# A hybrid decoder layer: where the convolution and gate of an up feature tile's second half stand in the queues

## The chip, the cores and the metric

The kernel runs on one core of a Trainium2 chip. The metric is the device time of one execution in microseconds (us); lower is better. The kernel before was timed three times: 1341.37, 1335.03 and 1337.39 us, median 1337.39.

## What is computed

One decoder layer on 16 learned tokens and 1024 input tokens of width 1024: RMSNorm, an input projection, four heads of differential attention beside four HGRN2 heads, an output projection, a residual sum, and then a feed-forward block with a causal convolution of width 3 over the tokens. The change lies in that last block, whose reference is:

```python
def conv_ffn(a, w_up, conv_w, conv_b, w_down):
    u = a @ w_up                                   # (1040, 1024) @ (1024, 2 * 2816)
    u = lax.conv_general_dilated(
        u, conv_w[:, None, :].astype(u.dtype), window_strides=(1,),
        padding=[(CONV_WIDTH - 1, 0)], dimension_numbers=('NWC', 'WIO', 'NWC'),
        feature_group_count=C) + conv_b            # each feature by itself: 3 taps over the tokens
    gate, up = jnp.split(u, 2, axis=-1)
    return (jax.nn.gelu(gate, approximate=True) * up) @ w_down
```

All data are 32-bit floats. The kernel writes every matmul operand as a high part and a low part and sums three products (high by high, high by low, low by high).

## The kernel before

**Feature tiles.** The 2816 gate features and the 2816 up features are taken in 22 tiles (`ft`) of 128 gate features and the 128 up features that belong to them. The tokens are taken in two halves of 512 (`p` = 0 and 1; half 0 has two more columns, the edge that the convolution needs). Tiles 0 and 1 go through `plain_unit`, tiles 2 to 21 through `unit`, which saves an eighth of the matmuls: it splits features, tokens and the model width in two each and forms seven products of sums where the plain way has eight. One product of one half is 12 matmuls into a bank of PSUM, over a weight part `uh` or `ul` and a token part `t`.

**The steps of a unit.** `unit` is a generator with seven steps, and the main loop at the end of the quoted code runs step j for half 0, then for half 1, before it goes on to step j + 1. So TensorE's order is pa, pa, pb, pb, pc, pc, pb, pb, pa, pa, pb, pb, pc, pc: bank pb is added to three times (steps 1, 3 and 5), and between two visits lie two groups of 12. Between the visits VectorE reads the bank: after step 1 it makes `u2` from pb, after step 3 `u3` from pb; both are called u in the profile. TensorE may add to pb again only when VectorE has read it. Step 3 of half 0 thus waits for the first `u2`, step 5 of half 0 for the first `u3`. `ug` (gate) and `uu` (up), 514 columns of one half, are filled in steps 3 to 6.

**Convolution and gate.** At the end of step 6 `gated` runs for that half. For the gate side and for the up side `conv` copies two columns from the half before (ScalarE), makes `c` with the third tap and the bias (ScalarE, ACTIVATE) and adds the other two taps (VectorE, two SCALAR_TENSOR_TENSOR). Then come the gelu of the gate side (ScalarE, ACTIVATE c<-c), the product of both sides (POOL, line 1280), and the store to `gsc` in DRAM (SP's queue, line 1281). The down projection later reads `gsc`.

**Weights.** In step j of tile ft, `prep` makes the parts of product j of tile ft + 1: loads into `ra` (line 1159), sums of weight blocks `ws` on POOL (line 1163), a cast to `uh` on ScalarE, and `ul` on VectorE or, for steps 2, 4 and 6, on POOL (line 155). A part is needed one tile after it is made, and its buffer is free when step j - 1 of the current tile is through.

**What sets the order.** TensorE's order is the program's. On the other engines a scheduler puts the instructions in order by priority when the kernel is built, and each engine runs its queue strictly in that order. `behind(name)` lets the instructions in its block be placed only behind a marked instruction of the same engine. Instructions of VectorE and ScalarE are recorded by a helper and have line 53 in the profile, so they are told apart by their tiles. Early in the up phase the first operands `gh` and `gl` of the down projection are made from `gi`, a load of `gsc`: two in the queues of tile 2 and one each in those of tiles 3 and 4.

Of the kernel before, what the change touches and what calls it, by code (L numbers as in the profile page):

```python
# [13 lines left out]
ALU = mybir.AluOpType  # L14
# [71 lines left out]
def layer_kernel(ctx: ExitStack, tc: tile.TileContext, x, meta, table, lbl, gpre, gpost, win,  # L86
# [17 lines left out]
    def close(*cms):  # L104
        for cm in cms:
            cm.__exit__(None, None, None)
# [957 lines left out]
    @contextmanager  # L1064
    def behind(*names):
        with ExitStack() as st:
            for nm in names:
                st.enter_context(tc.issue_after(marks[nm].ins))
            yield
# [191 lines left out]

    last = {}

    def conv(ft, p, side, u):
        m = ft + NF * side
        w = 2 * HALF
        if p:
            A.copy(u[:, :2], last[side][:, w:])
        last[side] = u
        c = cv.tile([P, w], F32, tag=f"c{side}", name=f"c{side}_{ft}_{p}", bufs=2 if side else 3)  # L1270
        A.activation(c, u[:, 2:2 + w], AF.Identity, bias=cbt[:, m:m + 1], scale=cwt[:, m, 2:3])
        V.scalar_tensor_tensor(c, u[:, 1:1 + w], cwt[:, m, 1:2], c, ALU.mult, ALU.add)
        V.scalar_tensor_tensor(c, u[:, 0:w], cwt[:, m, 0:1], c, ALU.mult, ALU.add)
        return c

    def gated(ft, p, ug, uu):
        cg = conv(ft, p, 0, ug)
        A.activation(cg, cg, AF.Gelu_apprx_tanh)
        cu = conv(ft, p, 1, uu)
        G.tensor_tensor(cg, cg, cu, op=ALU.mult)  # L1280
        st = SY.dma_start(gsc[P * ft: P * (ft + 1), 2 * HALF * p:2 * HALF * (p + 1)], cg)
        if ft == p == 0:
            marks["store"] = st

    def plain_unit(ft, p, bank):
        us = outputs(ft, p)
        e = EDGE[p]
        for col in range(2):
            a, n = ((2 - e, HALF + e), (2 + HALF, HALF))[col]
            for side in range(2):  # L1290
                pt = bank(f"pq{ft}_{p}_{col}{side}")[:, :n]
                for kh in range(2):
                    hi, lo = plain[ft, f"{side + 1}{kh + 1}"]
                    th, tl = tt[p][(0, 4, 7, 6)[2 * col + kh]]
                    for k in range(4):
                        s = slice(P * k, P * (k + 1))
                        T.matmul(pt, hi[:, s], th[:, k], start=(kh + k == 0), stop=False)
                        T.matmul(pt, hi[:, s], tl[:, k], start=False, stop=False)
                        T.matmul(pt, lo[:, s], th[:, k], start=False, stop=(kh == 1 and k == 3))
                A.copy(us[side][:, a:a + n], pt)  # L1300
                yield
        with behind("turned"):
            gated(ft, p, *us)
        yield

    def unit(ft, p, bank):
        nm = f"{ft}_{p}"
        ug, uu = outputs(ft, p)
        e = EDGE[p]
        x1 = xup.tile([P, HALF + 2], F32, tag="x1", name=f"x1_{nm}")[:, 2 - e:]  # L1310
        u2, u3 = (xup.tile([P, HALF], F32, tag=t, name=f"{t}_{nm}") for t in ("u2", "u3"))

        def mm(j, pt, first):
            hi, lo = made[7 * ft + j]
            th, tl = tt[p][j]
            pt = pt[:, HALF + e - width(p, j):]
            for k in range(4):
                s = slice(P * k, P * (k + 1))
                T.matmul(pt, hi[:, s], th[:, k], start=(first and k == 0), stop=False, skip_group_check=True)  # L1319
                T.matmul(pt, hi[:, s], tl[:, k], start=False, stop=False, skip_group_check=True)  # L1320
                T.matmul(pt, lo[:, s], th[:, k], start=False, stop=(k == 3), skip_group_check=True)  # L1321

        pa = bank(f"pa{nm}")[:, :HALF + e]
        mm(0, pa, True)
        A.copy(x1, pa)
        yield
        pb = bank(f"pb{nm}")[:, :HALF + e]
        mm(1, pb, True)
        V.tensor_tensor(u2, pb[:, e:], x1[:, e:], op=ALU.add)
        yield  # L1330
        pc = bank(f"pc{nm}")[:, :HALF + e]
        mm(2, pc, True)
        yield
        mm(3, pb, False)
        V.tensor_tensor(u3, pb[:, e:], x1[:, e:], op=ALU.add)
        V.tensor_tensor(uu[:, 2 + HALF:], pc[:, e:], u3, op=ALU.add)
        yield
        mm(4, pa, False)
        A.copy(ug[:, 2 - e:2 + HALF], pa)
        yield  # L1340
        mm(5, pb, False)
        V.tensor_tensor(uu[:, 2 - e:2 + HALF], pb, x1, op=ALU.add)
        yield
        mm(6, pc, False)
        V.tensor_tensor(ug[:, 2 + HALF:], pc[:, e:], u2, op=ALU.add)
        gated(ft, p, ug, uu)
        yield

    free = [ps_in("pq0"), ps_in("pq1")]
# [52 lines left out]
    for ft in range(2, NF):  # L1402
        units = [unit(ft, p, ps_b) for p in range(2)]
        for j in range(7):
            prep(7 * (ft + 1) + j)
            for u in units:
                next(u)
    close(t2_cm, t_cm, v_cm, xu_cm, mx_cm)

    f_cm, fp = pool("fin", 1)  # L1410
# [279 lines left out]
```

## Time and profile before

| | us |
|---|---|
| median of three runs | 1337.39 |
| the profiled execution | 1337.54 |
| its span in the trace | 1335.8 |
| TensorE busy | 1288.8 |
| VectorE busy | 914.6 |
| ScalarE busy | 690.3 |
| POOL busy | 414.1 |

The span runs from the first to the last instruction; 1.74 us of the profiled execution lie outside it. Times in the rows are us from the start of the span. A timeline row gives start, duration, engine, line, operation and tiles, with x and a count where rows in a row are merged; what stands in square brackets is the idle time of the engine ahead of it and what ended that. The names L1319, L1320 and L1321 are the three matmuls of a product in `unit`. The feature loop of `unit` runs from about 705 to 1113 us; 840 us is in tile 7, and a tile is about 19.9 us long.

### The profile page before, as it was taken

How to read it: one execution, taken by the hardware profiler on the slowest of the kernel's cores; microseconds unless marked ns; L12 is line 12 of the kernel's file. 1: busy time of each engine (PE TensorE's matmuls, PEld its weight loads, DVE VectorE, ACT ScalarE, POOL GpSimd, SP SyncE). 2: the span in 40 equal slices, each digit the busy share in tenths (PEclk: the TensorE clock that was granted, in tenths of full speed). 3: DMA queues.
4: the chain of work that ended last, by engine and by line, in shares of the span. 5: the costliest groups of instructions: out<-in, count | busy, mean ns of one | idle time of the engine just before them, and what ended most of it. 6: DMA issues, size and time to landing. Idle time of an engine off the chain costs nothing. (4 is left out here: it accounts for less than half of the span.)

```text
span 1335.8 us, 26319 instructions
## 1 busy us (share of the span) xinstructions
PE 1288.8 (96%) x10227; PEld 1191.1 (89%) x10227; DVE 914.6 (68%) x1589; ACT 690.3 (52%) x1670; POOL 414.1 (31%) x324
## 2 busy tenths in 40 slices
PE   6999999999999999999898999999999999999997
PEld 5898899989999999777798999999999998888886
DVE  7666657564756465836788787877777776697587
ACT  7365356534654565446655454454454454454454
POOL 3211211121202110122157566666657641010021
PEclk9999999999999999999998999999999999999999
DMA  6331333132311112826512222223222225964363
GB/s 215 108 125 60 104 101 122 52 128 92 115 36 34 32 33 66 259 96 231 187 64 88 95 73 82 84 76 115 80 82 78 80 80 177 330 218 154 107 205 119
DMA packets 84371, 153.07 MB, mean 115 GB/s; under 512 B 9571, under 2 KB 19843, under 8 KB 84246
## 3 DMA queue, kind: packets, MB, share of 16 engines
q1 hardware_dynamic: 84246, 151.39, 34.1%
q8 instruction: 80, 1.31, 0.4%
q14 instruction: 45, 0.37, 0.1%
HBM read 112.69 MB, written 38.67 MB: 113 GB/s over the span
## 5 line engine op out<-in xcount | busy, mean ns | idle before, releaser
L1319 PE MATMUL pb<-t,uh 128*128 128x258 f32 (+1 forms) x480 | 136.9, 285 | 8.1 <-DVE u L53 8.1
L1320 PE MATMUL pb<-t,uh 128*128 128x258 f32 (+1 forms) x480 | 135.6, 283 | 0.0
L1321 PE MATMUL pb<-t,ul 128*128 128x258 f32 (+1 forms) x480 | 135.6, 283 | 0.0
L1503 PE MATMUL pd<-wl,gh 128*128 128x512 f32 (+1 forms) x314 | 122.2, 389 | 0.3 <-DVE wl L53 0.2
L1504 PE MATMUL pd<-wh,gl 128*128 128x512 f32 (+1 forms) x314 | 122.1, 389 | 0.0
L1502 PE MATMUL pd<-wh,gh 128*128 128x512 f32 (+1 forms) x314 | 122.0, 388 | 0.0
L53 DVE SCALAR_TENSOR_TENSOR c<-uu,cwt,c 128x512 f32<-128x512 f32 x88 | 94.9, 1079 | 20.2 <-ACT c L53 19.5
L1280 POOL TENSOR_TENSOR c<-c,c 128x512 f32<-128x512 f32 x44 | 66.9, 1520 | 132.0 <-ACT c L53 123.6
L1319 PEld LDWEIGHTS pb<-t,uh 128*128 128x128 f32 x480 | 91.6, 191 | 9.2 <-DVE u L53 8.9
L1321 PEld LDWEIGHTS pb<-t,ul 128*128 128x128 f32 x480 | 92.0, 192 | 0.0
L1320 PEld LDWEIGHTS pb<-t,uh 128*128 128x128 f32 x480 | 91.4, 190 | 0.0
L1319 PE MATMUL pa<-t,uh 128*128 128x258 f32 (+1 forms) x320 | 90.2, 282 | 0.0
L1320 PE MATMUL pa<-t,uh 128*128 128x258 f32 (+1 forms) x320 | 89.9, 281 | 0.0
L1321 PE MATMUL pc<-t,ul 128*128 128x256 f32 x320 | 89.9, 281 | 0.0
L1319 PE MATMUL pc<-t,uh 128*128 128x256 f32 x320 | 89.9, 281 | 0.0
L1320 PE MATMUL pc<-t,uh 128*128 128x256 f32 x320 | 89.9, 281 | 0.0
L1321 PE MATMUL pa<-t,ul 128*128 128x258 f32 (+1 forms) x320 | 89.7, 280 | 0.0
L53 DVE SCALAR_TENSOR_TENSOR c<-ug,cwt,c 128x512 f32<-128x512 f32 x88 | 86.4, 982 | 1.8 <-ACT c L53 1.1
L1503 PEld LDWEIGHTS pd<-wl,gh 128*128 128x128 f32 x314 | 59.2, 189 | 13.9 <-DVE wl L53 1.0
L1504 PEld LDWEIGHTS pd<-wh,gl 128*128 128x128 f32 x314 | 59.3, 189 | 12.8
L1502 PEld LDWEIGHTS pd<-wh,gh 128*128 128x128 f32 x314 | 59.3, 189 | 12.8
L155 POOL TENSOR_TENSOR ul<-ws,uh 128x512 fp32r<-128x512 f32 x40 | 58.2, 1454 | 35.4 <-ACT uh L53 31.6
(411 smaller groups left out, 4205.2 us busy)
## 6 DMA issues: line engine op xcount, KB each, us to landing
ra<-in_wup_dram SPq DMA_DIRECT2D x80, 256.0 KB, 2.7
wd<-in_wdown_dram SPq DMA_DIRECT2D x44, 256.0 KB, 4.6
tsc<-wd SPq DMA_DIRECT2D x44, 256.0 KB, 2.9
gsc<-c SPq DMA_DIRECT2D x44, 256.0 KB, 2.0
wi<-tsc SPq DMA_DIRECT2D x44, 256.0 KB, 2.8
gi<-gsc SPq DMA_DIRECT2D x33, 256.0 KB, 3.6
wi<-in_wdown_dram SPq DMA_DIRECT2D x33, 256.0 KB, 3.4
msc<-mm SPq DMA_DIRECT2D x21, 256.0 KB, 3.5
```

The source lines that it names most:

```text
L53: ins = call(*args, **kw)
L155: (eng or G).tensor_tensor(lo, raw, hi.bitcast(F32), op=ALU.subtract)
L1280: G.tensor_tensor(cg, cg, cu, op=ALU.mult)
L1319: T.matmul(pt, hi[:, s], th[:, k], start=(first and k == 0), stop=False, skip_group_check=True)
L1320: T.matmul(pt, hi[:, s], tl[:, k], start=False, stop=False, skip_group_check=True)
L1321: T.matmul(pt, lo[:, s], th[:, k], start=False, stop=(k == 3), skip_group_check=True)
L1502: T.matmul(py, gh[:, s], wh, start=(k == 0 and pr not in (3, 7)), stop=False, skip_group_check=True)
L1503: T.matmul(py, gh[:, s], wl, start=False, stop=False, skip_group_check=True)
L1504: T.matmul(py, gl[:, s], wh, start=False, stop=(k == NH - 1), skip_group_check=True)
```

## The change

`seam` takes the copies of the two columns out of `conv`, so that they stay at the end of the half. The rest of `gated` for half 1 of tiles 2 to 21 goes on a list. `gate_waiting` runs what is on the list: after step 1 of the next tile has been issued, and placed behind that tile's last `u2` on VectorE; for the last tile, after the loop. Half 0 and the tiles of `plain_unit` keep their place.

```diff
+    def seam(p, us):
+        for side in range(2):
+            if p:
+                A.copy(us[side][:, :2], last[side][:, 2 * HALF:])
+            last[side] = us[side]
+
     def conv(ft, p, side, u):
         m = ft + NF * side
         w = 2 * HALF
-        if p:
-            A.copy(u[:, :2], last[side][:, w:])
-        last[side] = u
...
+    waiting = []
+
+    def gate_waiting():
+        with behind("u2"):
+            while waiting:
+                gated(*waiting.pop(0))
...
+        seam(p, us)
         with behind("turned"):
             gated(ft, p, *us)
...
-        V.tensor_tensor(u2, pb[:, e:], x1[:, e:], op=ALU.add)
+        marks["u2"] = V.tensor_tensor(u2, pb[:, e:], x1[:, e:], op=ALU.add)
...
-        gated(ft, p, ug, uu)
+        seam(p, (ug, uu))
+        if p:
+            waiting.append((ft, p, ug, uu))
+        else:
+            gated(ft, p, ug, uu)
         yield
...
             for u in units:
                 next(u)
+            if j == 1:
+                gate_waiting()
+    gate_waiting()
```

TensorE's instructions stand in the same order in both kernels. The order of the others is shown at the change from tile 5 to tile 6, which every later tile repeats. In the names c_5_1 is c of tile 5, half 1; the first u_6_0 and u_6_1 are `u2` of the halves of tile 6, the second u_6_0 is `u3` of half 0.

VectorE before, from the convolution of half 1 to the first `u3`:

```order
L53 SCALAR_TENSOR_TENSOR c_5_1_9446<-uu_1_9220,cwt,c_5_1_9446 128x512 x2
L53 SCALAR_TENSOR_TENSOR c_5_0_9415<-ug_0_9200,cwt,c_5_0_9415 128x512
L53 TENSOR_TENSOR ug_1_9219<-pc_1_9289,u_5_1_9222 128x256
L53 SCALAR_TENSOR_TENSOR c_5_0_9415<-ug_0_9200,cwt,c_5_0_9415 128x512
L53 TENSOR_TENSOR ul_9453<-ra_11_9454,uh_9452 128x512
L53 SCALAR_TENSOR_TENSOR c_5_1_9440<-ug_1_9219,cwt,c_5_1_9440 128x512 x2
L53 TENSOR_TENSOR ul_9505<-ws_9506,uh_9504 128x512
L53 TENSOR_TENSOR u_6_0_9469<-pb_0_9510,x_6_0_9468 128x256
L53 TENSOR_TENSOR u_6_1_9488<-pb_1_9524,x_6_1_9487 128x256
L53 TENSOR_TENSOR ul_9569<-ws_9570,uh_9568 128x512
L53 TENSOR_TENSOR u_6_0_9470<-pb_0_9510,x_6_0_9468 128x256
```

VectorE in the changed kernel, the same stretch (c_5_1_9527 is the gate side of half 1, c_5_1_9532 its up side):

```order
L53 SCALAR_TENSOR_TENSOR c_5_0_9415<-ug_0_9189,cwt,c_5_0_9415 128x512
L53 TENSOR_TENSOR ul_9442<-ra_11_9443,uh_9441 128x512
L53 SCALAR_TENSOR_TENSOR c_5_0_9415<-ug_0_9189,cwt,c_5_0_9415 128x512
L53 TENSOR_TENSOR ul_9494<-ws_9495,uh_9493 128x512
L53 TENSOR_TENSOR u_6_0_9458<-pb_0_9499,x_6_0_9457 128x256
L53 TENSOR_TENSOR u_6_1_9477<-pb_1_9513,x_6_1_9476 128x256
L53 SCALAR_TENSOR_TENSOR c_5_1_9527<-ug_1_9208,cwt,c_5_1_9527 128x512
L53 SCALAR_TENSOR_TENSOR c_5_1_9532<-uu_1_9209,cwt,c_5_1_9532 128x512
L53 SCALAR_TENSOR_TENSOR c_5_1_9527<-ug_1_9208,cwt,c_5_1_9527 128x512
L53 SCALAR_TENSOR_TENSOR c_5_1_9532<-uu_1_9209,cwt,c_5_1_9532 128x512
L53 TENSOR_TENSOR ul_9569<-ws_9570,uh_9568 128x512
L53 TENSOR_TENSOR u_6_0_9459<-pb_0_9499,x_6_0_9457 128x256
```

The four steps of half 1 have moved from ahead of the two `u2` to between them and the `ul` of step 3, which stands ahead of `u3`.

POOL before, around the two gate products:

```order
L1163 TENSOR_TENSOR ws_9570<-ra_11_9454,ra_21_9458 128x512
L1280 TENSOR_TENSOR c_5_0_9415<-c_5_0_9415,c_5_0_9420 128x512
L1280 TENSOR_TENSOR c_5_1_9440<-c_5_1_9440,c_5_1_9446 128x512
L155 TENSOR_TENSOR ul_9539<-ws_9462,uh_9538 128x512
L1163 TENSOR_TENSOR ws_9664<-ra_12_9460,ws_9506 128x512
L1163 TENSOR_TENSOR ws_9728<-ra_21_9724,ra_22_9722 128x512
L1163 TENSOR_TENSOR ws_9772<-ws_9728,ra_11_9720 128x512
```

POOL in the changed kernel, where the gate product is line 1283:

```order
L1163 TENSOR_TENSOR ws_9570<-ra_11_9443,ra_21_9447 128x512
L1283 TENSOR_TENSOR c_5_0_9415<-c_5_0_9415,c_5_0_9420 128x512
L155 TENSOR_TENSOR ul_9539<-ws_9451,uh_9538 128x512
L1163 TENSOR_TENSOR ws_9664<-ra_12_9449,ws_9495 128x512
L1163 TENSOR_TENSOR ws_9717<-ra_21_9713,ra_22_9711 128x512
L1283 TENSOR_TENSOR c_5_1_9527<-c_5_1_9527,c_5_1_9532 128x512
L1163 TENSOR_TENSOR ws_9761<-ws_9717,ra_11_9709 128x512
```

One `ul` and two `ws` have moved ahead of the product of half 1.

ScalarE before, from the cast of the first weights on:

```order
L53 CAST uh_9452<-ra_11_9454 128x512
L53 COPY x_6_0_9468<-pa_0_9471 128x258
L53 ACTIVATE c_5_1_9440<-ug_1_9219,cbt,cwt 128x512
L53 ACTIVATE c_5_0_9415<-c_5_0_9415 128x512
L53 COPY x_6_1_9487<-pa_1_9490 128x256
L53 CAST uh_9504<-ws_9506 128x512
L53 ACTIVATE c_5_1_9440<-c_5_1_9440 128x512
L53 CAST uh_9538<-ws_9462 128x512
L53 CAST uh_9568<-ws_9570 128x512
```

ScalarE in the changed kernel:

```order
L53 CAST uh_9441<-ra_11_9443 128x512
L53 ACTIVATE c_5_1_9527<-ug_1_9208,cbt,cwt 128x512
L53 COPY x_6_0_9457<-pa_0_9460 128x258
L53 ACTIVATE c_5_0_9415<-c_5_0_9415 128x512
L53 COPY x_6_1_9476<-pa_1_9479 128x256
L53 CAST uh_9493<-ws_9495 128x512
L53 CAST uh_9538<-ws_9451 128x512
L53 ACTIVATE c_5_1_9527<-c_5_1_9527 128x512
L53 CAST uh_9568<-ws_9570 128x512
```

The gelu of half 1 has gone behind one cast (step 2's weights) and still stands ahead of the cast of step 3's. On SP's queue the order is the same at this place; in tiles 3 and 4 the load `gi` has gone ahead of the store of half 1.

## The prediction

> **What bounds the kernel now.** I read the page first, then TensorE's waits by stage, then the timelines of all engines over one feature tile. The page gives TensorE nearly the whole span:
>
> ```profile
> PE 1288.8 (96%) x10227; PEld 1191.1 (89%) x10227; DVE 914.6 (68%) x1589; ACT 690.3 (52%) x1670; POOL 414.1 (31%) x324
> ```
>
> The change acts from tile 3 on, which begins after 724 us. What TensorE waits for is listed for the up phase from 640 us, and then again from 724 us alone:
>
> ```profile
> PE pb L1319 <- DVE u L53: 8.1, 4, 6.3
> ...
> PE pb L1319 <- DVE u L53: 1.8, 3, 0.7
> ```
>
> Of the 8.1 us, 6.3 are one wait in tile 2, before any gate of `unit` has been moved. What the change can still reach is three waits of 1.8 us. In the stage's steady part TensorE is never idle (columns: window, length, then busy time of PE, PEld, DVE, ACT and POOL):
>
> ```profile
> 800.00:1080.00 280.00, 280.00 (x2371) 279.81 (x2370) 214.40 (x311) 138.44 (x269) 180.41 (x127) 1.00 0.25 84
> ```
>
> The clock is granted in full there (1.00), and VectorE is busy for 214 of 280 us. So this stage is bound by TensorE's own rate, with a few nicks, all at the start of a pb group:
>
> ```profile
> 761.89 0.28 PE L1321 MATMUL pc<-t,ul 128*128 128x256 f32 x1
> 762.84 0.39 PE L1319 MATMUL pb<-t,uh 128*128 128x256 f32 x1 [0.66 <-DVE u L53]
> 763.06 0.28 PE L1320 MATMUL pb<-t,uh 128*128 128x256 f32 x1
> ...
> 769.25 0.40 PE L1319 MATMUL pb<-t,uh 128*128 128x258 f32 x1 [0.56 <-DVE u L53]
> ...
> 784.22 0.39 PE L1319 MATMUL pb<-t,uh 128*128 128x256 f32 x1 [0.54 <-DVE u L53]
> ...
> 823.93 0.37 PE L1319 MATMUL pb<-t,uh 128*128 128x256 f32 x1
> 824.13 0.28 PE L1320 MATMUL pb<-t,uh 128*128 128x256 f32 x1
> ...
> 1062.38 0.37 PE L1319 MATMUL pb<-t,uh 128*128 128x256 f32 x1
> ```
>
> Those at 762.84 and 784.22 follow a pc group: step 3 waits for `u2`. The one at 769.25 follows pa (its group has 258 columns): step 5 waits for `u3`, behind the down projection's `gl`. From 823.93 to 1062.38 every second tile, seven in all and 39.7 us apart (so a tile is 19.9 us long), shows a small catch at `u2`: no idle time, but a first matmul of 0.37 instead of 0.28.
>
> **What the change removes.** At a free start matmuls follow each other by 0.12 us (763.06 is 0.22 after 762.84, the catch; the rest by 0.12). At 762.84 the step is 0.95 instead of 0.12, so 0.83 are lost, 0.17 more than the idle time printed, and 0.10 with the next one: 0.93. At 784.22 by the same rule 0.54 + 0.17 + 0.10 = 0.81. The seven catches cost 0.20 - 0.12 = 0.08 each, 0.6 together. All of it hangs on `u2`: 0.93 + 0.81 + 0.6 = 2.3 us. It goes if `u2` comes earlier by 0.8 us or more.
>
> VectorE over one such tile shows what `u2` stands behind:
>
> ```profile
> 835.49 2.23 DVE L53 SCALAR_TENSOR_TENSOR c<-uu,cwt,c 128x512 f32<-128x512 f32 x2
> 837.64 0.74 DVE L53 SCALAR_TENSOR_TENSOR c<-ug,cwt,c 128x512 f32<-128x512 f32 x1
> 838.30 0.41 DVE L53 TENSOR_TENSOR ug<-pc,u 128x256 f32<-128x256 f32 x1
> ...
> 839.29 0.68 DVE L53 TENSOR_TENSOR ul<-ra,uh 128x512 fp32r<-128x512 f32 x1
> 839.89 2.44 DVE L53 SCALAR_TENSOR_TENSOR c<-ug,cwt,c 128x512 f32<-128x512 f32 x2
> 842.26 0.68 DVE L53 TENSOR_TENSOR ul<-ws,uh 128x512 fp32r<-128x512 f32 x1
> 842.86 0.74 DVE L53 TENSOR_TENSOR u<-pb,x 128x256 f32<-128x256 f32 x2
> 844.65 1.52 DVE L53 TENSOR_TENSOR ul<-ws,uh 128x512 fp32r<-128x512 f32 x1 [1.05 <-ACT uh L53]
> 846.10 0.41 DVE L53 TENSOR_TENSOR u<-pb,x 128x256 f32<-128x256 f32 x1
> ...
> 838.20 0.28 PE L1319 MATMUL pb<-t,uh 128*128 128x258 f32 x1
> ...
> 841.04 0.28 PE L1319 MATMUL pc<-t,uh 128*128 128x256 f32 x1
> ...
> 843.87 0.28 PE L1319 MATMUL pb<-t,uh 128*128 128x256 f32 x1
> ...
> 849.54 0.28 PE L1319 MATMUL pb<-t,uh 128*128 128x258 f32 x1
> ```
>
> The last four rows are TensorE's dates: pb of step 1 from 838.20 to 841.04 for both halves, step 3 from 843.87, step 5 from 849.54. The first `u2` ends at 842.86 + 0.41 = 843.27, 0.6 ahead of its date. By the order before, the pairs at 835.49 and 839.89 are the four convolution steps of half 1; the change takes them from in front of it.
>
> **What it adds: the same four between `u2` and `u3`.** Here POOL decides. POOL's and ScalarE's rows of the same stretch:
>
> ```profile
> 834.77 1.62 POOL L1163 TENSOR_TENSOR ws<-ra,ra 128x512 f32<-128x512 f32 x1
> 840.22 1.57 POOL L1280 TENSOR_TENSOR c<-c,c 128x512 f32<-128x512 f32 x1 [3.83 <-ACT c L53]
> 843.08 1.30 POOL L1280 TENSOR_TENSOR c<-c,c 128x512 f32<-128x512 f32 x1 [1.29 <-ACT c L53]
> 844.33 1.30 POOL L155 TENSOR_TENSOR ul<-ws,uh 128x512 fp32r<-128x512 f32 x1
> 845.71 1.62 POOL L1163 TENSOR_TENSOR ws<-ra,ws 128x512 f32<-128x512 f32 x1
> ...
> 835.66 0.82 ACT L53 ACTIVATE c<-ug,cbt,cwt 128x512 f32<-128x512 f32 x1 [1.01 <-DMA ra<-in_wup_dram]
> 836.46 0.62 ACT L53 CAST uh<-ra 128x512 fp32r<-128x512 f32 x1
> 837.04 0.38 ACT L53 COPY x<-pa 128x258 f32<-128x258 f32 x1
> 842.37 0.63 ACT L53 ACTIVATE c<-c 128x512 f32<-128x512 f32 x1 [1.46 <-DVE c L53]
> 844.00 0.62 ACT L53 CAST uh<-ws 128x512 fp32r<-128x512 f32 x1 [0.49 <-PE pc L1320]
> ```
>
> VectorE's `ul` takes 0.68 alone (839.29), but 1.52 at 844.65, where POOL runs from 844.33 to 845.63: it ends at 846.17, 0.54 after POOL. POOL's next, begun at 845.71, takes 1.62 instead of 1.30. The `u` at 846.10, which reads PSUM, keeps its 0.41 beside it. So a VectorE instruction with both operands in SBUF and a POOL instruction go one after the other, and the one held ends about 0.54 after POOL. The Trainium skill says the same in "SBUF — State Buffer", section "SBUF: two separate sides": the two share a port pair under an exclusive lock, and whoever starts first has it for the whole instruction. The rows agree. By that rule the moved steps lose the shelter that they have now: ahead of the gate product POOL sits idle for 3.83 us, in which they run; behind `u2` its queue is full.
>
> I lay the tile out again by these durations, in the new order. The gate sum of half 1 (`ug`, now at 838.30) no longer stands behind the convolution and is free at 835.6, when its bank is complete: two groups of 1.42 ahead of 838.20, and 0.2 to 0.3 more, since the last matmul is 0.28 long and begins 0.12 before the next group. ScalarE makes c of half 0 by 836.48, then a cast, then c of half 1 by 837.8. VectorE's two steps of half 0 run from 836.5 and 837.8, alone, since POOL's `ws` is over at 836.39. The gelu follows at 838.5, POOL's product from 839.2 to 840.5. The `ul` of step 1's weights (cast over by about 840.0) is held behind it to 841.05. The first `u2` runs from 841.0 to 841.4, 1.9 earlier than now; the second, free when its group is over (841.04 and 0.3 by the same count), to 841.7. The 2.3 us go.
>
> Now the four. The first runs from 841.7 to 842.4, alone. POOL's `ul`, whose cast must wait for step 1's last matmul (841.04) and is over by 841.8, comes in behind it; the second is held to 843.95, the third behind `ws` to 845.6, the fourth behind the other `ws` to 847.25. The gelu of half 1 goes after the third, to 846.3; the cast of step 3's weights stands behind it, to 846.9; their `ul` on VectorE runs 847.2 to 847.9, since POOL has just taken up the product. The first `u3` ends at 848.2. TensorE wants it at 849.5: 1.3 us to spare, in this parity of tiles. In the other `u2` is now 0.5 later against TensorE (its catches), so about 0.8 to spare. I therefore put the cost at nothing: 19 tiles (3 to 21) hide it behind the matmuls of steps 3 and 4. If the cover goes, each loses what `u3` is late.
>
> **The two tiles with `gl`.** Its rows:
>
> ```profile
> 767.58 1.28 DVE L53 TENSOR_TENSOR gl<-gi,gh 128x512 fp32r<-128x512 f32 x1 [3.16 <-ACT gh L53]
> 768.78 0.41 DVE L53 TENSOR_TENSOR u<-pb,x 128x256 f32<-128x256 f32 x1
> ```
>
> Here VectorE waited 3.16 us for a load that SP had queued behind the store of half 1. In the new order it stands ahead of that store, and the product of half 0 is 1 us earlier, so the wait shrinks; in its place `gl` comes after the four. It adds 0.7 to 1.6 ahead of `u3`, whose spare time is 0.8 to 1.3: between nothing and 0.8 lost, against 0.56 + 0.17 + 0.10 = 0.83 now in tile 4. I take the middle, about 0.4 in each of the two tiles, which equals the 0.83: no change, with 0.8 either way.
>
> **The other queues moved past.** POOL makes the product of half 1 at about 847.3 instead of 843.08, and one `ws` sum and what follows move back by up to a product's 1.30; they make weights for the next tile, 19.9 us on. SP stores half 1 some 4 us later, at 848.7:
>
> ```profile
> 841.82 2.91 SPq L1281 DMA_DIRECT2D gsc<-c  x2
> 851.34 0.88 SPq L1159 DMA_DIRECT2D ra<-in_wup_dram  x2
> ```
>
> The next load in that queue goes out at 851.34 and isn't held up. `ug` and `uu` of half 1 are read until 847.25; ScalarE overwrites that buffer after step 4 of half 1, behind 849.5. The copies of two columns only leave `conv`. The last tile's gate, after the loop, stands in the order where it stood, so the start of the down projection is unchanged.
>
> **Sum.** 1337.5 (the profiled execution) - 2.3 + 0 = 1335.2 us. The median, 1337.4, lies 0.15 below that execution, which changes nothing. This is 0.2% faster; about 0.5%, 6.7 us here, is what a measurement can tell from no change, so I forecast "the same".
>
> **The rivals.**
> *No gain.* The waits of 2.3 us come back at `u3`, for instance 0.1 us in each of 19 tiles and 0.4 more in the two with `gl`: 2.7 us. For it speaks that spare time of 0.8 is less than one more hold (about 0.9); against it that 0.8 is still spare. About 1337.9.
> *Slower: POOL holds all five.* In my layout POOL holds three of the five SBUF instructions (the four and the `ul`) between `u2` and `u3`. If it holds all five, each takes about 1.6 (the second of the pair at 839.89 took 2.44 - 0.74 = 1.7, the `ul` 1.52): 841.7 + 8.0 + 0.4 = 850.1, 0.6 after 849.5. Nineteen tiles lose 11 us: 1337.5 - 2.3 + 11 = 1346. It decides from two more holds in a tile. For it speaks the exclusive order in the rows; against it that POOL's next instruction after the two `ws` is the product, which must wait for the fourth step itself, so that POOL pauses just there.
> *More gain.* The 6.3 us in tile 2 go as well. The rows of the queues up to that place are the same in both kernels, so nothing shortens the wait. 1335.2 - 6.3 = 1329.
>
> **Chances.** Forecast 0.73, no gain 0.14, slower 0.10, more gain 0.03. Range: the runs before reached 2.4 below and 4.0 above their median; from 1335.2 that and the 0.8 of `gl` give 1332.0 to 1340.0, and for a part of the holds (0.1 to 0.2 a tile) I go on to 1341.0; the slower case lies outside. Faster by over 0.5% holds the last rival and a little of the scatter, 0.04; slower 0.10; the same 0.86.
>
> **What would show it.** Right: TensorE's waits from 724 us fall from 1.8 to under 1 us, none of them after a pc group; POOL's idle time ahead of its gate products falls, its product of half 1 comes about 4 us later in the tile; `u2` ends some 2 us ahead of step 3; the wait of 6.3 us stays. Wrong: a wait of TensorE at pb after a pa group in every tile, behind VectorE steps of 1.5 us and more; or TensorE waiting for `uh` or `ul`; or a feature tile whose length isn't 19.8 to 19.9 us.

## The result, and the profile after

Four runs of the changed kernel gave 1347.55 to 1357.81 us, median 1352.61; four of the kernel before 1335.03 to 1341.50, median 1339.38. The ratio is 1.0106 (95% interval 1.0067 to 1.0144): slower by about 1.1%, where the forecast was 0.2% faster. The profiled execution took 1347.55 us, with a span of 1345.7.

The feature loop alone shows more than the span. Its first matmul and the first of the down projection, in the trace of before:

```profile
705.22 0.29 PE L1319 MATMUL pa<-t,uh 128*128 128x258 f32 x1
...
1113.44 0.40 PE L1502 MATMUL pd<-wh,gh 128*128 128x512 f32 x1
```

The same two in the trace of after:

```profile
700.50 0.29 PE L1330 MATMUL pa<-t,uh 128*128 128x258 f32 x1
...
1123.42 0.40 PE L1520 MATMUL pd<-wh,gh 128*128 128x512 f32 x1
```

That is 408.2 us before and 422.9 after: 14.7 more. The span grew by 9.9 only, because this execution reached the loop 4.7 us earlier. That start lies between 700 and 710 us in the traces of this study, whatever is done inside the loop, so the loop's length is used below beside the ratios. (Counted from these starts, the tile shown at 840 us is tile 8 in both kernels, not tile 7.)

TensorE's waits from 724 us in the changed kernel (us in all, times, longest):

```profile
PE pb L1330 <- DVE u L53: 13.4, 17, 1.0
```

and its steady window (columns as in the prediction):

```profile
800.00:1080.00 280.00, 268.50 (x2252) 265.67 (x2251) 220.30 (x296) 124.96 (x254) 176.44 (x122) 1.00 0.24 79
```

TensorE, idle for nothing in this window before, is idle for 11.5 of 280 us at the same clock of 1.00. From 724 us on, all these waits lie at one place of the tile, between steps 4 and 5:

```profile
838.87 0.28 PE L1330 MATMUL pc<-t,uh 128*128 128x256 f32 x1
...
847.25 0.28 PE L1332 MATMUL pa<-t,ul 128*128 128x256 f32 x1
848.42 0.40 PE L1330 MATMUL pb<-t,uh 128*128 128x258 f32 x1 [0.88 <-DVE u L53]
```

The pa group ends at 847.25, and the pb group (258 columns: step 5) starts 1.17 us later instead of 0.12: 1.05 lost, and 0.1 more with the next matmul; counted over the whole tile it is 1.01. It waits for `u3`, as the prediction named the sign of being wrong. A tile lasts 20.86 us instead of 19.85 (from the first pa matmul of one tile to that of the next).

VectorE's queue up to that `u3`, as in the tile shown of before:

```profile
832.97 1.45 DVE L53 SCALAR_TENSOR_TENSOR c<-uu,cwt,c 128x512 f32<-128x512 f32 x1
834.34 0.74 DVE L53 TENSOR_TENSOR ug<-pc,u 128x256 f32<-128x256 f32 x2
...
839.18 1.11 DVE L53 TENSOR_TENSOR ul<-ws,uh 128x512 fp32r<-128x512 f32 x1 [1.48 <-ACT uh L53]
840.21 0.74 DVE L53 TENSOR_TENSOR u<-pb,x 128x256 f32<-128x256 f32 x2
840.88 1.12 DVE L53 SCALAR_TENSOR_TENSOR c<-ug,cwt,c 128x512 f32<-128x512 f32 x1
841.92 1.78 DVE L53 SCALAR_TENSOR_TENSOR c<-uu,cwt,c 128x512 f32<-128x512 f32 x1
843.62 1.78 DVE L53 SCALAR_TENSOR_TENSOR c<-ug,cwt,c 128x512 f32<-128x512 f32 x1
845.32 0.74 DVE L53 SCALAR_TENSOR_TENSOR c<-uu,cwt,c 128x512 f32<-128x512 f32 x1
846.61 1.42 DVE L53 TENSOR_TENSOR ul<-ws,uh 128x512 fp32r<-128x512 f32 x1 [0.55 <-ACT uh L53]
847.95 0.41 DVE L53 TENSOR_TENSOR u<-pb,x 128x256 f32<-128x256 f32 x1
```

POOL beside it:

```profile
838.44 1.30 POOL L1283 TENSOR_TENSOR c<-c,c 128x512 f32<-128x512 f32 x1 [2.87 <-ACT c L53]
839.74 1.70 POOL L155 TENSOR_TENSOR ul<-ws,uh 128x512 fp32r<-128x512 f32 x1
841.52 1.62 POOL L1163 TENSOR_TENSOR ws<-ra,ws 128x512 f32<-128x512 f32 x1
843.23 1.62 POOL L1163 TENSOR_TENSOR ws<-ra,ra 128x512 f32<-128x512 f32 x1
846.19 1.29 POOL L1283 TENSOR_TENSOR c<-c,c 128x512 f32<-128x512 f32 x1 [1.34 <-ACT c L53]
```

The first three of the four moved steps and the `ul` behind them overlap POOL's instructions and take 1.12, 1.78, 1.78 and 1.42; the fourth is free and takes 0.74. The sums that read PSUM keep their 0.41. The Trainium skill, "SBUF — State Buffer", section "Who interferes with whom", has it so: a VectorE instruction with two SBUF inputs contends with one of GpSimd (POOL here) that reads SBUF; one with at most one SBUF input, outside the 2-port performance modes, does not. The rows agree, and their price here is up to 1.04 us for an instruction of 0.74.

Last, what the chain of waits consists of over one such tile, by engine and line. Before, from 826 to 848 us:

```profile
by line: PE pb L1320 14.5%; PE pb L1319 14.5%; PE pb L1321 14.5%; PE pa L1319 10.9%; PE pa L1321 10.2%; PE pa L1320 10.2%; PE pc L1319 8.6%; PE pc L1320 8.6%; PE pc L1321 8.6%
```

After, from 826.5 to 848.3 us, from one tile's late `u3` to the next one's:

```profile
by line: DVE c L53 29.3%; DVE ul L53 23.9%; issue 15.5%; ACT c L53 10.6%; ACT uh L53 7.8%; DVE u L53 6.2%; DVE uu L53 5.1%; DVE ug L53 1.9%; ACT ug L53 1.7%; ACT x L53 1.2%; ACTq L53 0.4%; ACT uu L53 0.2%
```

Before, the chain is TensorE alone. After, TensorE isn't on it at all: a whole tile runs from `u3` over `uu`, the casts, `ul`, the convolution of half 0, `ug`, `u2`, the moved steps, gelu, cast and `ul` to the next `u3`, on VectorE and ScalarE, with POOL's holds inside VectorE's durations. The view infers what released what, so it gives a theory and not yet a proof; the later experiments tried it.

### The profile page after: what moved, and what is told of

Its sections match the earlier page's. It is cut to its first block, busy times and chain, and to the rows that moved or that the text cites. A ratio compares the mean times of both kernels' runs of the same rounds, so it can differ in the third digit from the quotient of the medians.

```text
span 1345.7 us, 26302 instructions
## 1 busy us (share of the span) xinstructions
PE 1290.2 (96%) x10227; PEld 1190.2 (88%) x10227; DVE 935.3 (70%) x1589; ACT 684.3 (51%) x1670; POOL 420.2 (31%) x324
## 4 chain that ended last, share of the span: by engine, by line
PE 45%; DVE 22%; ACT 11%; issue 6%; DMA 2%; POOL 1%; SPq 1%; ACTq 0%; DVEq 0%; POOLq 0%
DVE c L53 9%; PE pd L1521 5%; PE pd L1522 5%; PE pd L1520 5%; DVE ul L53 5%; ACT c L53 3%; PE pa L708 2%; ACT uh L53 2%; PE py L969 2%; PE py L973 2%; PE py L971 2%; DVE uu L53 1%; DVE u L53 1%; DMA wd<-in_wdown_dram 1%; PE pt L684 1%
## 5 line engine op out<-in xcount | busy, mean ns | idle before, releaser
L53 DVE SCALAR_TENSOR_TENSOR c<-uu,cwt,c 128x512 f32<-128x512 f32 x88 | 100.8, 1146 | 19.6 <-ACT c L53 19.5
L53 DVE SCALAR_TENSOR_TENSOR c<-ug,cwt,c 128x512 f32<-128x512 f32 x88 | 93.8, 1065 | 11.5 <-ACT c L53 11.4
L1283 POOL TENSOR_TENSOR c<-c,c 128x512 f32<-128x512 f32 x44 | 62.4, 1418 | 114.3 <-ACT c L53 102.6
L53 ACT ACTIVATE c<-c 128x512 f32<-128x512 f32 x44 | 27.8, 632 | 121.6 <-DVE c L53 121.6
L155 POOL TENSOR_TENSOR ul<-ws,uh 128x512 fp32r<-128x512 f32 x40 | 61.0, 1526 | 49.3 <-ACT uh L53 49.1
L53 DVE TENSOR_TENSOR ul<-ws,uh 128x512 fp32r<-128x512 f32 x40 | 50.4, 1261 | 36.2 <-ACT uh L53 35.9
```

The costliest lines, as they stand in the source:

```text
L53: ins = call(*args, **kw)
L155: (eng or G).tensor_tensor(lo, raw, hi.bitcast(F32), op=ALU.subtract)
```

## The experiments

The loop and tile lengths were read from each trace as above (a tile: the usual one between 800 and 1080 us). The ratios are to the kernel before.

| version | loop | tile | ratio (95%) |
|---|---|---|---|
| before | 408.2 | 19.85 | 1 |
| changed | 422.9 | 20.86 | 1.0106 (1.0067 to 1.0144) |
| POOL's order put back | 408.3 | 20.09 | 0.9995 (0.9983 to 1.0006) |
| `ul` of step 3 behind `u3` | 407.1 | 19.85 | 0.9990 (0.9978 to 1.0003) |
| the same, more rounds | 406.6 | 19.85 | 0.9994 (0.9983 to 1.0006) |
| only the gate side moved | 416.5 | 20.45 | 1.0056 (1.0040 to 1.0072) |
| gate behind `u3` | 415.9 | 20.39 | 1.0064 (1.0043 to 1.0084) |
| cast ahead of the gelu | 410.2 | 20.17 | 1.0023 (1.0009 to 1.0037) |
| changed, step 6 shortened | 417.0 | 20.7 | profiled once |
| before, step 6 shortened | 386.9 | 18.90 | profiled once |
| gate side alone, POOL's order put back | 413.5 | 20.31 | 1.0044 (1.0028 to 1.0060) |
| two sums of POOL left out | 405.8 | 19.85 | profiled once |
| one tile further back | 405.3 | 19.85 | 0.9981 (0.9970 to 0.9992) |
| the same, `gl` behind `u3` | 404.1 | 19.85 | 0.9960 (0.9948 to 0.9972) |

The first four were judged by three theories. H: POOL's `ul` and two `ws` hold the moved steps and the `ul` of step 3. R1: what costs is the place of `u3` behind that `ul`, whose cast stands behind the gelu of half 1. R2: the other engines have more work than a tile lasts, wherever the steps stand.

**POOL's order put back.** POOL's product of half 1 stands again right behind that of half 0, with the rest of the orders as in the changed kernel.

```
...
+            with behind("product") if ft > 2 and j != 3 else nullcontext():
+                prep(7 * (ft + 1) + j)
-            prep(7 * (ft + 1) + j)
```

The rest of the edit keeps `u3` behind the `ul` of step 3, so that VectorE's order stays.

> The changed kernel with one thing undone: POOL's order. The product of half 1 comes again right behind that of half 0, and one ul and two ws sums behind it; VectorE's and ScalarE's orders stay those of the changed kernel. Theory H (the four moved steps and the ul of step 3 are held by POOL's ul and ws): the steps take 0.74 each, u3 is in time, TensorE waits under 0.2 us a tile, the loop from the first matmul of tile 2 to the down projection takes 406 to 409 us instead of 422.9, and the time is within 0.3% of the kernel before. Rival R1 (what delays u3 is its place behind that ul, whose cast stands behind the gelu of half 1): the order on those two engines is the same, so the wait stays near 1 us a tile and the loop at 421 to 424. Rival R2 (the three side engines have more work than a tile lasts, wherever the steps stand): the loop stays above 418.

VectorE and POOL in that version:

```profile
842.76 0.74 DVE L53 SCALAR_TENSOR_TENSOR c<-ug,cwt,c 128x512 f32<-128x512 f32 x1
843.42 0.74 DVE L53 SCALAR_TENSOR_TENSOR c<-uu,cwt,c 128x512 f32<-128x512 f32 x1
844.09 0.74 DVE L53 SCALAR_TENSOR_TENSOR c<-ug,cwt,c 128x512 f32<-128x512 f32 x1
844.75 0.74 DVE L53 SCALAR_TENSOR_TENSOR c<-uu,cwt,c 128x512 f32<-128x512 f32 x1
```

```profile
845.62 1.29 POOL L1283 TENSOR_TENSOR c<-c,c 128x512 f32<-128x512 f32 x1 [3.99 <-ACT c L53]
```

All four steps are free again, because POOL stands idle for 3.99 us ahead of its product, and the whole loss is gone: 408.3. (Of the tile's 20.09 in the later tiles, 0.24 is a catch at `u2`.) R1 is out as a cause by itself: `u3` stands at the same place behind the same gelu. So is R2.

**The `ul` of step 3 behind `u3`.**

```
-            prep(7 * (ft + 1) + j)
+            if j != 3:
+                prep(7 * (ft + 1) + j)
...
+            if j == 3:
+                with behind("u3"):
+                    prep(7 * (ft + 1) + j)
```

> The changed kernel with the ul of step 3's weights placed behind u3 on VectorE; the four moved steps and POOL's ul and two ws stay where the change has them. H: the four are still held, 1.1 to 1.8 us each, but u3 no longer pays for the gelu, the cast and the held ul, 2 us or more; it ends about 1 us ahead of step 5, the wait goes to under 0.3 us a tile, loop 406 to 411 us. R1: the wait goes wholly, with the steps no longer than 0.74 needed for that; loop 406 to 408. R2: loop above 418.

Its steady window, and VectorE's last moved step with what follows:

```profile
800.00:1080.00 280.00, 280.00 (x2373) 280.00 (x2372) 230.98 (x312) 137.96 (x271) 191.71 (x127) 1.00 0.26 86
```

```profile
827.70 1.78 DVE L53 SCALAR_TENSOR_TENSOR c<-uu,cwt,c 128x512 f32<-128x512 f32 x1
829.41 0.41 DVE L53 TENSOR_TENSOR u<-pb,x 128x256 f32<-128x256 f32 x1
```

The loss is gone here as well, although the steps are still held (1.78 for the last) and VectorE is busy for as long in a tile as in the changed kernel: 16.4 us in both (230.98 x 19.85 / 280 here, 220.30 x 20.86 / 280 there), against 15.2 before. So the holds cost nothing as a sum. They cost where they stand in a chain that ends in a dated sum; here `u3` waits for neither gelu, cast nor `ul`. Both H and R1 allowed this result.

**Only the gate side moved.** The up side's two steps stay at the end of the half.

```
...
-            waiting.append((ft, p, ug, uu))
+            waiting.append((ft, p, ug, uu, conv(ft, p, 1, uu)))
```

> Half of the change: the up side's two steps of half 1 stay ahead of u2 as before, the gate side's two steps, the gelu, the product and the store move behind u2 as in the change. H: two held steps instead of four between u2 and u3, about 3 us less, so u3 is in time; u2 also is early by the two that moved; wait under 0.2 us a tile, loop 406 to 409 us, time within 0.3% of before. R1: gelu, cast and ul are still in front of u3; about half of the wait stays, 0.4 to 0.6 us a tile, loop 414 to 418. R2: loop above 418.

TensorE's waits from 724 us:

```profile
PE pb L1330 <- DVE u L53: 8.0, 16, 0.9
```

A miss for H: with two steps less in that place, over half of the loss stays (416.5). R1's number came, but the run with POOL's order put back had left it no ground. That was the sign that neither theory, both of which looked only at what stands between `u2` and `u3`, had the whole path.

**The whole gate behind `u3`.**

```
-        with behind("u2"):
+        with behind("u3"):
...
-            if j == 1:
+            if j == 3:
```

> The same moved gate, but issued after step 3 and placed behind the tile's last u3 instead of its last u2, so that no sum with a date stands behind the four steps for two groups of pc. H: the steps may be held by POOL (1.1 to 1.8 us each) and it costs nothing; u2 and u3 are both in time, loop 405 to 408 us (before 408.2), time 0 to 3 us under the kernel before. R1: the same. R2: loop above 418, because the work of a tile is what it was.

Its VectorE rows, the last moved step and what stands behind it:

```profile
854.00 0.73 DVE L53 SCALAR_TENSOR_TENSOR c<-uu,cwt,c 128x512 f32<-128x512 f32 x1
854.77 0.42 DVE L53 TENSOR_TENSOR uu<-pc,u 128x256 f32<-128x256 f32 x1
```

A second miss for H, and one for R1, which expected the same. No date lies close behind the four steps now, yet 415.9 us: TensorE waits 17 times, 7.0 us, each time for the next tile's `u2` behind a pc group. What the steps delay is `uu`, with it the convolution of half 0, with that `u2`. From here on two theories stood against each other: the loop theory (a chain through VectorE, ScalarE and POOL that closes from tile to tile and has outgrown TensorE's tile) and the place theory (`u3` is late by what stands behind `u2`, and TensorE paces `u2`).

**Step 6 shortened, in both kernels.** Left out of the computation in these two: in the last product of each unit the four of twelve matmuls that multiply high weights with low tokens. This makes TensorE's tile 0.94 us shorter and leaves the order between `u2` and `u3` as it was.

```
...
+                if j != 6:
+                    T.matmul(pt, hi[:, s], tl[:, k], start=False, stop=False, skip_group_check=True)
-                T.matmul(pt, hi[:, s], tl[:, k], start=False, stop=False, skip_group_check=True)
```

> The changed kernel with part of the computation left out: in the last product of each unit (step 6) the 4 of its 12 matmuls that multiply high weights with low tokens. TensorE's work of a tile is shorter by 8 x 0.118 = 0.94 us, at a place that lies neither between u2 and u3 nor ahead of a date of theirs in the same tile. Loop theory: TensorE is not on the chain that sets the tile, so the 20.9 us of a tile stay, the loop takes 420 to 424 us as in the changed kernel (422.9), and the wait at u3 grows from about 1 to about 2 us a tile. Place theory (u3 is late by what stands between u2 and u3, and u2 is paced by TensorE): the wait stays at about 1 us a tile and the loop gets shorter by what was left out, 20 x 0.94 = 18.9: 403 to 405.

> The kernel before with the same matmuls left out. If TensorE alone sets its tile the loop falls by 18.9 from 408.2 to about 389.3. Both theories have TensorE as the bound there, so both expect a fall; the loop theory adds that the other engines' chain must be the next bound, somewhere between 18.9 and 19.9 us a tile: 389 to 400, and says how near the kernel before stood to it.

Two of TensorE's waits, and the chain from 820 to 862 us, in the shortened changed kernel:

```profile
813.71 0.39 PE L1330 MATMUL pb<-t,uh 128*128 128x258 f32 x1 [1.62 <-DVE u L53]
...
834.42 0.39 PE L1330 MATMUL pb<-t,uh 128*128 128x258 f32 x1 [1.53 <-DVE u L53]
```

```profile
by line: DVE c L53 42.0%; DVE ul L53 22.3%; ACT uh L53 8.1%; issue 8.0%; ACT c L53 7.0%; DVE u L53 4.8%; DVE uu L53 4.1%; DVE ug L53 2.5%; ACT ug L53 1.7%; ACT x L53 1.2%; ACTq L53 0.3%; ACT uu L53 0.2%
```

The steady window of the shortened kernel before:

```profile
800.00:1080.00 280.00, 280.00 (x2373) 280.00 (x2372) 197.76 (x330) 146.79 (x283) 200.01 (x131) 1.00 0.27 88
```

With 0.94 us less of TensorE's work in a tile, the changed kernel's tile lasts 834.42 - 813.71 = 20.71 us, 0.15 less than its 20.86; the idle time ahead of step 5 takes up the rest.

The edit did more than shorten TensorE's work, though: in both shortened kernels the scheduler also gave VectorE and ScalarE another order ahead of `u2`. For the changed kernel the rows tell the two effects apart. The `u3` of one tile in the changed kernel (its `ug`, `u2` and next `u3` are shown above, at 834.34, 840.21 and 847.95):

```profile
827.09 0.41 DVE L53 TENSOR_TENSOR u<-pb,x 128x256 f32<-128x256 f32 x1
```

The same turn in its shortened form:

```profile
813.24 0.41 DVE L53 TENSOR_TENSOR u<-pb,x 128x256 f32<-128x256 f32 x1
...
820.49 0.74 DVE L53 TENSOR_TENSOR ug<-pc,u 128x256 f32<-128x256 f32 x2
821.16 1.11 DVE L53 TENSOR_TENSOR ul<-ra,uh 128x512 fp32r<-128x512 f32 x1
822.20 1.52 DVE L53 SCALAR_TENSOR_TENSOR c<-ug,cwt,c 128x512 f32<-128x512 f32 x2
...
826.23 0.74 DVE L53 TENSOR_TENSOR u<-pb,x 128x256 f32<-128x256 f32 x2
...
833.96 0.41 DVE L53 TENSOR_TENSOR u<-pb,x 128x256 f32<-128x256 f32 x1
```

From `u3` to `ug` both take 7.25 us, and from `u2` to the next `u3` 7.74 and 7.73. Only from `ug` to `u2` do they differ, 5.87 and 5.74, and there a `ul` now stands ahead of both convolution steps of half 0 instead of between them. So the stretches that kept their order did not get shorter at all with less work of TensorE.

The shortened kernel before follows TensorE all the way, to 18.90 a tile, and is not idle even then. Its loop, 386.9, lies below the 389 that both theories gave as the least, because 2.0 us of the waits behind tile 2 went as well. But its VectorE makes both `ug` sums first and runs the four gate steps in one row:

```profile
828.40 0.74 DVE L53 TENSOR_TENSOR ug<-pc,u 128x256 f32<-128x256 f32 x2
...
830.71 2.73 DVE L53 SCALAR_TENSOR_TENSOR c<-ug,cwt,c 128x512 f32<-128x512 f32 x4
```

So the other engines can do a tile in 18.9 us in that order. For the order of the kernel before no run shows more than that they keep up with TensorE's 19.85. The chain lasts 20.7 to 20.9 us in the changed kernel, so the change made it longer by at least 0.9. The place theory is out (404 expected, 417.0 measured). The loop theory's own number was 3 too high: the loop is 5.9 shorter than the changed kernel's, of which 1.7 lie in tile 2, ahead of the steady chain, 0.9 in the last tile, which has no wait, and 3.3 in the 18 tiles between.

**Cast ahead of the gelu.** On ScalarE the cast of step 3's weights goes ahead of the gelu of half 1; the other queues stay.

```
...
+            if j == 3 and half:
+                with behind("uh"):
+                    gelu_product(*half.pop(0))
...
```

> The changed kernel with one pair exchanged on ScalarE: the gelu of half 1 stands behind the cast of step 3's weights instead of ahead of it. The orders of VectorE and POOL are those of the changed kernel, so the same four steps stand between u2 and u3 beside the same work of POOL. By the loop theory, a chain through VectorE, ScalarE and POOL alone (from one tile's u3 over uu, casts, ul, c, ug, u2, the four steps, gelu, cast and ul to the next tile's u3) lasts 20.9 us where TensorE needs 19.9: it gets shorter by the gelu (about 0.6) and by the hold of that ul (1.42 - 0.68 = 0.7, since the product would no longer run just then), comes to 19.6 and lets go: 406 to 410 us from the first matmul of tile 2 to the down projection, about 1338 in all. By the theory that the held steps decide, three of four stay held: 418 to 423, about 1345 and more. Below 402, or TensorE waiting for u2 in every tile, would fit neither.

```profile
846.11 0.68 DVE L53 TENSOR_TENSOR ul<-ws,uh 128x512 fp32r<-128x512 f32 x1
...
849.21 1.77 DVE L53 TENSOR_TENSOR ul<-ra,uh 128x512 fp32r<-128x512 f32 x1 [0.84 <-ACT uh L53]
```

The `ul` ahead of `u3` is free again (0.68 for 1.42) and comes without the 0.55 of idle time, as expected; but the next `ul` now meets POOL's own `ul`, and takes 1.77 for 1.10. The tile comes to 20.17 instead of the expected 19.6, and the loop to 410.2, just outside the 406 to 410. Most of the loss went by a shorter link of the chain, with three of the four steps held as before; the new hold took back a part.

**Gate side alone, POOL's order put back.** The version with only the gate side moved, with the edit of the first experiment.

> The version in which only the gate side of half 1 moves (416.5 us for the loop), with POOL's product of half 1 put back right behind that of half 0, so that POOL stands idle while VectorE does the two steps; VectorE's and ScalarE's orders are unchanged. Loop theory: the two steps fall from 1.11 + 1.67 to 2 x 0.74, so the chain of 20.3 gets shorter by 1.3, to 19.0, below TensorE's 19.9: 406 to 410, about 1338 in all. If it was the place of the up side's steps (ahead of u2) that made u2 and then u3 late, POOL's order changes nothing: 414 to 418, about 1346.

VectorE at the end of the tile:

```profile
833.61 1.80 DVE L53 SCALAR_TENSOR_TENSOR c<-uu,cwt,c 128x512 f32<-128x512 f32 x1 [0.94 <-ACT c L53]
...
835.67 1.44 DVE L53 SCALAR_TENSOR_TENSOR c<-uu,cwt,c 128x512 f32<-128x512 f32 x1
...
837.37 3.15 DVE L53 SCALAR_TENSOR_TENSOR c<-uu,cwt,c 128x512 f32<-128x512 f32 x2
```

A miss for the number of the loop theory: 413.5, against 416.5 without the edit and 406 to 410 expected. The two moved steps are free (1.52 for both) and the waits at step 5 are gone; but POOL's work, put off behind its product, now meets the up side's four steps of both halves (1.80, 1.44 and 3.15 for two), `ug` and then `u2` come late, and TensorE waits 0.3 behind pc. The rival of this run, that the place of the up side's steps ahead of `u2` makes it late, was right on where; that POOL's order changes nothing was wrong. In this version the chain of waits does pass through TensorE, for steps 3 and 4, as it does not in the changed kernel.

**Two sums of POOL left out.** The changed kernel, with the two `ws` that hold the second and third step left out of the computation from tile 4 on (raw blocks stand in for the sums). VectorE's and ScalarE's orders are unchanged.

```
-            w_sum("1", raws["21"], raws["22"], ALU.add)
+            if ft > 3:
+                sums["1"] = raws["21"]
+            else:
+                w_sum("1", raws["21"], raws["22"], ALU.add)
...
-            src = w_sum("4", raws["12"], sums["2"], ALU.subtract)
+            src = raws["12"] if ft > 3 else w_sum("4", raws["12"], sums["2"], ALU.subtract)
```

> The changed kernel with two of POOL's weight sums of each tile left out from tile 4 on (the two ws that stand ahead of its product of half 1; raw blocks go into the matmuls in their place). VectorE's and ScalarE's orders are those of the changed kernel. If POOL's two ws are what lengthens the chain, the second and third of the four steps fall from 1.78 to 0.74 each: 20.9 - 2.1 = 18.8 us a tile, less than TensorE's 19.85, so the waits at u3 vanish and the loop comes to 406 to 409 us. If the chain is long by the number of VectorE's and ScalarE's instructions alone, it stays at 418 to 423.

```profile
843.08 1.39 DVE L53 SCALAR_TENSOR_TENSOR c<-ug,cwt,c 128x512 f32<-128x512 f32 x1
844.39 0.74 DVE L53 SCALAR_TENSOR_TENSOR c<-uu,cwt,c 128x512 f32<-128x512 f32 x1
845.06 0.74 DVE L53 SCALAR_TENSOR_TENSOR c<-ug,cwt,c 128x512 f32<-128x512 f32 x1
```

The second and third step take 0.74, the first is still held by POOL's `ul`, and TensorE has no wait left from 724 us: 405.8, a hair below the 406 to 409 expected. The same VectorE and ScalarE instructions in the same order thus cost 17 us more in the loop or nothing, by what POOL does beside them. (POOL has two instructions less in the whole tile here, and two casts no longer wait for a sum, so this run doesn't say at which of the places they cost. The run with POOL's order put back leaves nothing out and agrees.)

**One tile further back, and more rounds of the version before it.** With the `ul` of step 3 behind `u3`, the gate of half 1 of tile 1 waits too, behind `u2` of tile 2, where the wait of 6 us had stayed; `gl` goes behind `u3` of tile 2.

```
-        with behind("turned"):
-            gated(ft, p, *us)
+        if ft and p:
+            waiting.append((ft, p, *us))
+        else:
+            with behind("turned"):
+                gated(ft, p, *us)
...
-        split(gh, gl, a, V)
+        with behind("u3_2_1"):
+            split(gh, gl, a, V)
```

> The version that stood at 0.999 (the ul of step 3 behind u3), carried one tile further back: the gate of half 1 of tile 1 waits as well, behind u2 of tile 2, and gl of the down projection goes behind u3 of tile 2. By the loop theory nothing changes from tile 3 on (19.85 us a tile). In tile 2 the first u2 stood 6.6 us late behind a row of VectorE steps, of which the four of half 1 took 1.75 + 0.75 + 0.75 + 0.74 = 4.0: the wait falls to 2 to 3 us, the loop from 407.1 to 402.5 to 404.5, the time to 0.995 to 0.998 of the kernel before. If the four steps come late for u3 of tile 2 in place of u2, or POOL's rows there hold them (up to 1.8 each), the wait moves to step 5 and the loop stays at 406 to 408.

> The same kernel as in the run with the ul of step 3 behind u3, for a narrower interval, beside the version that goes one tile further. Loop theory: TensorE's waits of 2.3 us in the kernel before are gone and nothing comes in their place: 0.997 to 0.9995 of the kernel before, loop 406 to 408. If the gain is lost elsewhere: 0.9995 to 1.001.

The wait in tile 2 fell from 6.6 us to 3.1, by 3.5 of the 4.0 expected. Tile 2 itself got shorter by 6.3, from 29.46 to 23.17. After the wait of 6.6 us the granted clock was 0.50 from 723 to 728 us, and matmuls followed each other by 0.21 us instead of 0.12; after that of 3.1 us it was 1.00 from 716 to 721. But from 724 us on, where the version before had 0.4 us of waits, there are now 4.5, 1.7 of them at `u2` of tile 3, 1.8 at its step 5 and 1.1 at step 5 of tile 4, so the loop got to 405.3 and not to the expected 402.5 to 404.5. The version before it, at 0.9994 over more rounds, can't be told from the kernel before; its loop is 1.6 us shorter in that trace, of the 2.3 that I had counted.

**The same, with `gl` behind `u3` in tiles 3 and 4 too.**

```
+        with behind({(1, 2): "u3_3_1", (1, 3): "u3_4_1"}.get((pr, k), "u3_2_1")):
-        with behind("u3_2_1"):
```

> The version that goes one tile further back (loop 405.3, ratio 0.9981), with gl of the down projection behind u3 in tiles 3 and 4 too. In tile 3 u3 stood behind gl, whose cast came after that of the weights: u3 should come about 1.5 us earlier there and a wait of about 1.4 at step 5 go. The wait for u2 in tile 2 (3.1) and that in tile 3 (1.7) stay. Loop 403.5 to 404.5, 0.9965 to 0.9985 of the kernel before. If gl only moves the wait to the sum behind it, the loop stays at 405 to 406.

TensorE's waits from 640 us in this version:

```profile
PE pb L1333 <- DVE u L53: 4.5, 3, 3.2
```

The loop is 404.1, and the time 0.9960 (0.9948 to 0.9972) of the kernel before, the loop as expected and the time just below the 0.9965 to 0.9985, but in part by luck. The wait at `u2` of tile 3, which was to stay at 1.7, went as well (0.1 is left); in its place 0.7 and 0.6 stand at `u2` of tiles 4 and 5, and tile 2 got 1.7 longer (24.88 for 23.17), with the clock at 0.66 for the 5 us behind its wait. This version beats both kernels, the one by 0.4% and the other by 1.4% (0.9960 / 1.0106).

## Why the prediction was wrong

**The step that failed** is the sentence "I therefore put the cost at nothing: 19 tiles (3 to 21) hide it behind the matmuls of steps 3 and 4", with the 1.3 us of spare time (0.8 in the other parity) on which it rests. Counted from the end of step 1's matmuls (841.04 in the layout, 838.87 in the trace), TensorE's date for step 5 was right: 8.5 us in both (849.5, and 847.25 + 0.12). But `u2` was done 0.7 us behind that end in the layout (841.7) and 2.1 in the trace (840.21 + 0.74), and from there to the end of `u3` I had 6.5 us (848.2 - 841.7) where it took 7.4 (847.95 + 0.41 - 840.95). In sum 1.4 + 0.9 = 2.3 us later, so 1.3 to spare became 1.0 late.

**The 0.9: which instructions POOL holds.** I held the second, third and fourth step and left the first and the `ul` free. POOL's `ul` came in ahead of the first step, not behind it; the fourth was free; and the `ul` was held by the product (1.42 for 0.68), after 0.55 of idle time behind gelu and cast. The sentence "POOL pauses just there" was right on the pause and wrong on whom it shelters. Nor were the four steps all sheltered before: the rows of the pairs at 835.49 and 839.89 last 2.23 and 2.44 us where two free steps take 1.41 (844.09 + 0.74 - 843.42, with POOL's order put back), so one of each pair was held there too. The rival "slower: POOL holds all five" is what happened in kind: four of five held, and waits at step 5 in every tile from 3 to 19. That its 1346 lies so near the profiled 1347.55 us is luck: it had the tiles lose 11 us where they lost 16.7, and this execution reached the loop 4.7 us early. It had a chance of 0.10, and its mark ("two more holds in a tile") was too far off: one more was enough.

**The 1.4: a layout against TensorE's clock alone.** I let `ug` start when its bank was complete, two groups ahead of step 1 and 0.2 more: 836.03 - 2.84 + 0.2 = 833.4 in the trace's times. The second `ug` began at about 834.7 (834.34 + 0.34), behind a step held to 1.45 us at 832.97. The layout covered one tile, and began with side engines that were on time. A late `u3` delays `uu`, that the convolution of half 0, and so the next `u2`: the start of the layout hangs on its own end. That this loop, without TensorE, sets the tile is shown by the shortened step 6, with the chain view beside it; in the kernel before the same engines keep up with TensorE's 19.85 us.

**What held.** TensorE did bound this stage before, with little in reserve but some waits for `u2`; those did go (from 724 us on no wait behind a pc group is left in the changed kernel). They were nearer 1.8 us than 2.3: tiles 3 to 21 of the kernel before are 2.7 us longer than 19 times 19.85, of which 0.83 is the wait behind `gl`. `u2` came early for step 3, by 0.8 (840.95 against 838.87 + 2.84) instead of the 2 named as a sign. The wait in tile 2 stayed (6.1 for 6.3). The order of SP's queue and the stores cost nothing that shows. The cost of `gl` in tiles 3 and 4 can't be told apart from the loss in every tile. The sum should have had 17 us where it had nothing: tiles 3 to 21 of the changed kernel are 16.7 us longer than 19 times 19.85, against 2.7 before, and with 0.65 more in tile 2 that makes the loop's 14.7.

**What stays open.** POOL's holds were moved and taken away, not measured at each place by themselves; how the 2.3 us of the layout divide in a steady loop, where each link delays all the others, is an account of one tile. Why the loop starts anywhere between 700 and 710 us was not tried.

## What to carry to other kernels

Before calling a moved step covered, lay out not one stretch but a whole turn: start from the late sum, follow it through the other engines to the same sum in the next tile, with the holds at their new places, and compare that length with the bounding engine's tile. The slack of a single wait says little about it; leaving a little of the bounding engine's work out shows on the chip how long the other chain is, once one has looked whether the other queues kept their order. An idle POOL ahead of an instruction that waits for VectorE can be what keeps VectorE's steps short; moving either one's work moves the holds elsewhere, and what decides is whether a dated result stands behind them.

## What the runs showed of the hardware

An SBUF-to-SBUF step of VectorE of 0.74 us takes 1.78 between POOL instructions that follow each other closely, and POOL's own 1.30 become 1.62 to 1.70: each is held in turn, and both get slower. Held time alone does not set the time: VectorE is busy for 16.4 us of a tile both in the changed kernel, at a loop of 423 us, and in the version with the `ul` behind `u3`, at 407; in the kernel before it is 15.2 at 408. The long wait in tile 2 cost more than itself: after its 6.3 us in the kernel before, the granted clock was 0.54 from 720 to 725 us, and some twenty matmuls started 0.21 us apart instead of 0.12. After waits of about 1 us in the changed kernel the clock stayed at 1.00; after 3.1 and 3.2 us in the last two versions it was 1.00 in the one and 0.66 in the other, so these runs give no length from which it falls. TensorE's tile, once it was unhindered, repeated to 0.01 us from tile to tile (19.85, or 18.90 with 8 matmuls less).
